# Seven-product feed-forward tiles: each product tied behind the one before it on the tensor engine

## The chip, the core and the metric

The kernel runs on one core of a Trainium2 chip. The metric is the device time of one execution in microseconds (us), as the median of three runs. The engines have short names in the profile: PE is the tensor engine (matrix products, called "products" here; PEld is its weight load), DVE the vector engine, ACT the scalar engine, POOL and SP the two engines that issue the transfers. Each engine works through a queue of its own in order and waits where an operand isn't ready.

## What is computed

One decoder layer on 512 tokens of width 1024, in float32: a SwiGLU feed-forward, a mixer (dilated attention beside a gated recurrence), and a second SwiGLU feed-forward, each between RMS norms. Only the feed-forwards matter here. The hidden width D_FF is 2816.

```python
def swiglu(x, w_gate, w_up, w_down):
    return (jax.nn.silu(x @ w_gate) * (x @ w_up)) @ w_down

f = swiglu(rms_norm(h, ffn1_norm_pre[l]), ffn1_w_gate[l], ffn1_w_up[l], ffn1_w_down[l])
h = h + 0.5 * rms_norm(f, ffn1_norm_post[l])
...
f = swiglu(rms_norm(h, ffn2_norm_pre[l]), ffn2_w_gate[l], ffn2_w_up[l], ffn2_w_down[l])
h = h + 0.5 * rms_norm(f, ffn2_norm_post[l])
```

## The kernel before

**Precision.** A float32 operand is split into a high and a low part (`split`, L269 on ACT for the high part, L270 on DVE for the low part), and a product of two operands is three matmuls: high by high, high by low, low by high. In a gate/up product these are L1008, L1009 and L1010, in a down step L922, L923 and L924. L923 is the first that needs the low part of the down weights, L1010 the first that needs the low part of the gate/up weights.

**Gate/up tiles.** The hidden width is cut into 22 tiles of 128 columns, numbered f = 0 to 21. In the first feed-forward tiles 0 to 5, in the second 0 to 3, are made by plain products. For each of the others, `prod` makes gate and up together by a scheme of seven half-size products instead of eight (a Strassen-like form): p1, p5, p6, p2, p7, p3, p4 in the order of the code, each 4 blocks of 128 by 3 matmuls, 12 matmuls of 256 columns. They accumulate in three banks of PSUM. Bank `b` (bank_73 or bank_74, by turns) takes p1, p6, p7 and p4; bank `y` (bank_75) a copy of `b` after p1 and then p2; bank `z` (bank_78) p5 and then p3. Between them ACT copies a bank out (`copy`, L1016, and L1029 for `b` to `y`) and DVE adds (`sum_of`, L1021): p6 and p7 may start only when the earlier content of `b` is copied, p3 only when p5's content of `z` is copied out, and p4 only when DVE has added p7's content of `b`.

**Down windows.** The down product is taken by seven products too, over groups of four tiles, called window groups a = 0 to 3. Its seven steps (`step`, L922 to L924, each 2 halves j = 0, 1 of 6 matmuls of 512 columns) run between the gate/up tiles in windows of one, two or three steps, listed in WINDOWS and LEAD. p1, p6, p7, p4 accumulate in bank_76 and bank_77, p2, p5, p3 in bank_79 and bank_80; after a step DVE adds a bank into the accumulator `facc` (L941, L939) or ACT copies it (L934). Three windows of the first feed-forward matter below: group 0's (p1, p2, p5) after tile 7, group 1's (p1, p2, p5) after tile 10 and group 1's (p6, p7) after tile 11. The down weights of the first two steps of a window are made (`down_form`: L269 on ACT, L270 on DVE) in the tile before it, behind that tile's last copy, by the edge `behind("copy")`; the third step's weights are made in the window.

**What sets the order.** A list scheduler places each engine's instructions by priority and by its own estimate of when operands are ready. The code can hold it with edges: `behind("PE")` makes what is traced in it come after the PE instruction noted last, in the order of the PE's queue. An edge on one engine's own queue costs no semaphore. Before, the first product of a tile (p1) and each down step had such an edge, and p5, p6, p2, p7, p3, p4 had none.

```python
            with behind("PE"):
                product("p1", b, True)
            ...
            product("p5", z, True)
            c5 = copy(z)
```

Of the kernel before, what the change touches and what calls it, by code (L numbers as in the profile page):

```python
# [154 lines left out]
def hybrid_layer(ctx: ExitStack, tc: tile.TileContext, xT: bass.AP, xN: bass.AP, wst: bass.AP,  # L155
                 first: bass.AP, rows: bass.AP, wdn: bass.AP, wbig: bass.AP, consts: bass.AP, bias: bass.AP, out: bass.AP):
    nc = tc.nc
    DVE, ACT, PE = nc.vector, nc.scalar, nc.tensor
# [121 lines left out]
    def tmp(name):  # L280
        return tpool.tile([P, T], F32, name=name, tag="t")
# [534 lines left out]
    def ffn(n, x, r, forms_x, home, pss):  # L816
# [80 lines left out]
        def down_form(a, p):  # L897
            w = wdt[home.n % 2]
            home.n += 1
            split(w[:, 0, :], w[:, 1, :], at[p])  # L900
            ready[p] = w
            q = NEXT[p]
            a += p in ("p7", "p3", "p4")
            if a < SEVEN:
                supply(a, q)
# [80 lines left out]
        @contextmanager  # L986
        def behind(*engines):
            with ExitStack() as es:
                for e in engines:
                    if e in last:  # L990
                        es.enter_context(tc.issue_after(last[e]))
                yield

        def prod(f, w, due):

            g = tmp("g")
            b, y, z = b_of[f % 2][:, :HB], y_[:, :HB], z_[:, :HB]
            u = ub[:, f % 4, :] if 4 < f < LAST[0] else tmp("u")
            if n == 1 and f in (6, 8):
                u = tmp("u")  # L1000

            def product(p, ps, start):
                if len(t[p][0].shape) == 4:
                    ps = ps.rearrange("q (b t) -> q b t", b=2)
                for k in range(4):
                    ks = slice(k * P, (k + 1) * P)
                    wh, wl, xh, xl = w[p][:, 0, ks], w[p][:, 1, ks], t[p][0][:, k], t[p][1][:, k]
                    PE.matmul(ps, wh, xh, start=start and k == 0, stop=False, skip_group_check=True)  # L1008
                    PE.matmul(ps, wh, xl, start=False, stop=False, skip_group_check=True)  # L1009
                    i = PE.matmul(ps, wl, xh, start=False, stop=k == 3, skip_group_check=True)  # L1010
                last["PE"] = i.ins

            def copy(ps):
                c = tpool.tile([P, HB], F32, name="c", tag="c", bufs=CB)
                with tc.high_priority(offset=EVAC):
                    last["copy"] = ACT.activation(c, ps, AF.Copy).ins  # L1016
                return c

            def sum_of(dst, ps, c):
                with tc.high_priority(offset=EVAC):  # L1020
                    DVE.tensor_add(dst, ps, c)  # L1021

            lead = f == n0
            with behind("PE"):
                product("p1", b, True)
            c1 = copy(b) if lead else None
            if not lead:
                with tc.high_priority(offset=EVAC):
                    ACT.activation(y, b, AF.Copy)  # L1029
            product("p5", z, True)  # L1030
            c5 = copy(z)
            product("p6", b, False)
            c6 = copy(b)
            product("p2", y, lead)
            if lead:
                sum_of(g[:, lo_], y, c1)
            with behind("copy"):
                for a, p in due:
                    down_form(a, p)
            product("p7", b, False)  # L1040
            sum_of(u[:, hi_], b, c5)
            with tc.high_priority(offset=EVAC):
                ACT.activation(g[:, lo_], g[:, lo_] if lead else y, AF.Silu)
            product("p3", z, False)
            sum_of(g[:, hi_], z, c6)
            product("p4", b, False)
            last["ACT"] = ACT.activation(g[:, hi_], g[:, hi_], AF.Silu).ins
            with tc.high_priority(offset=EVAC):
                DVE.scalar_tensor_tensor(u[:, lo_], g[:, lo_], -1.0, b, op0=ALU.mult, op1=ALU.mult)
            last["DVE"] = DVE.scalar_tensor_tensor(u[:, hi_], g[:, hi_], -1.0, u[:, hi_], op0=ALU.mult,  # L1050
                                                   op1=ALU.mult).ins
            return u
# [41 lines left out]
        for at_, ev in enumerate(order):  # L1094
# [16 lines left out]
            elif ev[0] == "prep":  # L1111
                with behind("DVE", "ACT"):
                    forms[ev[1]] = w_forms_in_place(("gu", n, ev[1]))
            elif ev[0] == "prod":
                due = order[at_ + 1]
                u = prod(ev[1], forms.pop(ev[1]), [(due[1], p) for p in due[2][:2]] if due[0] == "window" else [])
                if ev[1] == 4:
                    part0(u)
            elif ev[0] == "finish":
                finish(ev[1], u)  # L1120
            else:
                for i, p in enumerate(ev[2]):
                    with behind("PE"):
                        step(ev[1], p)
                    if len(ev[2]) > 2 and i == 0:
                        down_form(ev[1], ev[2][2])
# [612 lines left out]
```

## Time and profile before

| | before |
|---|---|
| median of three runs (lowest, highest) | 1225.02 us (1224.43 to 1225.36) |
| the profiled execution itself | 1224.49 us |
| span of the trace in it | 1222.7 us |
| PE busy | 1211.8 us, 99%, 7682 matmuls |
| DVE busy | 972.4 us, 80% |
| ACT busy | 736.5 us, 60% |
| granted clock of the tensor engine | 0.999 |
| the chain that ended last | PE 94%, DVE 4%, issue 1%, ACT 1% |

Matmuls are pipelined, so a matmul's row shows a longer time than it takes of the engine: rows of 0.28 us (256 columns) start 0.12 us after one another, rows of 0.39 us (512 columns) 0.23 us after one another. What the engine lost in a wait is therefore read from the starts.

### The profile page before, as it was taken

Reading aid. Unit: us, or ns where it says so; the run is one execution under the profiler, and the core shown is the slowest. Engines: PE = TensorE matmul, PEld = TensorE weight load, DVE = VectorE, ACT = ScalarE, POOL = GpSimd, SP = SyncE. Lnnn points to the kernel's source line nnn. Section 1 sums busy time; section 2 is a strip of 40 time slices with the busy share of each in tenths; the row PEclk is TensorE's granted clock in tenths of the full one; section 3 lists DMA queues with packets and bytes.
Section 4 is the critical chain, followed back from the end, with each engine's and each line's share of the span. In section 5 each row is a group of like instructions: output and inputs, shape, how many; then the busy total and the mean of one; then the engine's idle time right before and its main releaser. Section 6 shows DMA issues by size and latency. Waiting matters only on the chain.

```text
span 1222.7 us, 19286 instructions
## 1 busy us (share of the span) xinstructions
PE 1211.8 (99%) x7682; PEld 1099.0 (90%) x7682; DVE 972.4 (80%) x1513; ACT 736.5 (60%) x1221; POOL 82.1 (7%) x135
## 2 busy tenths in 40 slices
PE   9999999999999999999999999999999999999998
PEld 8888989999878899999998888888899999999996
DVE  7998778988579887888766798755788887979864
ACT  6566665665656564656665787724556665656552
POOL 0001101010102000000000000000110010101000
PEclk9999999999999999999999999999999999999999
DMA  6336546464735322222244234324463655555441
GB/s 247 138 104 172 162 115 166 136 166 127 253 122 175 107 81 102 78 79 104 70 140 151 88 121 155 129 99 164 143 190 108 162 154 147 156 139 160 117 155 69
DMA packets 37130, 166.57 MB, mean 136 GB/s; under 512 B 4144, under 2 KB 7600, under 8 KB 25008
## 3 DMA queue, kind: packets, MB, share of 16 engines
q1 hardware_dynamic: 18432, 107.13, 25.0%
q0 software_dynamic: 18608, 58.20, 18.0%
q8 instruction: 60, 0.98, 0.3%
q14 instruction: 30, 0.25, 0.1%
HBM read 153.26 MB, written 7.86 MB: 132 GB/s over the span
## 4 chain that ended last, share of the span: by engine, by line
PE 94%; DVE 4%; issue 1%; ACT 1%; DMA 0%; DVEq 0%; ACTq 0%
PE bank L1008 9%; PE bank L1009 9%; PE bank L1010 9%; PE bank L285 8%; PE bank L284 8%; PE bank L286 8%; PE bank L675 5%; PE bank L676 5%; PE bank L677 5%; PE bank L923 4%; PE bank L922 4%; PE bank L924 4%; PE bank L405 3%; PE bank L406 3%; PE bank L404 3%; DVE w L270 1%
## 5 line engine op out<-in xcount | busy, mean ns | idle before, releaser
L270 DVE TENSOR_TENSOR w<-raw,w 128x1024 fp32r<-128x1024 f32 (+1 forms) x272 | 297.0, 1102 | 69.1 <-ACT w L269 63.3
L269 ACT ACTIVATE w<-raw 128x1024 fp32r<-128x1024 f32 (+1 forms) x272 | 255.6, 959 | 97.0 <-PE bank L286 38.2
L1008 PE MATMUL bank<-big,w 128*128 128x256 f32 x816 | 233.9, 287 | 3.1 <-DVE u L1021 1.3
L1009 PE MATMUL bank<-big,w 128*128 128x256 f32 x816 | 230.7, 283 | 0.0
L1010 PE MATMUL bank<-big,w 128*128 128x256 f32 x816 | 229.4, 283 | 0.0
L1008 PEld LDWEIGHTS bank<-big,w 128*128 128x128 f32 x816 | 156.2, 191 | 8.3 <-DVE u L1021 2.0
L1009 PEld LDWEIGHTS bank<-big,w 128*128 128x128 f32 x816 | 156.3, 192 | 1.5
L1010 PEld LDWEIGHTS bank<-big,w 128*128 128x128 f32 x816 | 155.7, 192 | 0.0
L922 PE MATMUL bank<-wd,act 128*128 128x512 f32 x224 | 87.8, 392 | 0.0
L923 PE MATMUL bank<-wd,act 128*128 128x512 f32 x224 | 87.7, 392 | 0.0
L924 PE MATMUL bank<-wd,act 128*128 128x512 f32 x224 | 87.3, 390 | 0.0
L284 PE MATMUL bank<-big,w 128*128 128x512 f32 x176 | 68.5, 389 | 0.0
L285 PE MATMUL bank<-big,w 128*128 128x512 f32 x176 | 68.5, 389 | 0.0
L286 PE MATMUL bank<-big,w 128*128 128x512 f32 x176 | 68.5, 389 | 0.0
L675 PE MATMUL bank<-big,w 128*128 128x256 f32 x228 | 66.1, 290 | 0.0
L677 PE MATMUL bank<-big,w 128*128 128x256 f32 x228 | 64.7, 284 | 0.0
L286 PE MATMUL bank<-act,w 128*128 128x512 f32 (+1 forms) x184 | 64.7, 352 | 0.0
L285 PE MATMUL bank<-act,w 128*128 128x512 f32 (+1 forms) x184 | 64.7, 352 | 0.0
L284 PE MATMUL bank<-act,w 128*128 128x512 f32 (+1 forms) x184 | 64.6, 355 | 0.0
L676 PE MATMUL bank<-big,w 128*128 128x256 f32 x228 | 64.5, 283 | 0.0
L1016 ACT ACTIVATE c<-bank 128x256 f32<-128x256 f32 x70 | 26.6, 382 | 61.4 <-PE bank L1010 61.0
L270 DVE TENSOR_TENSOR wd<-npair,wd 128x1024 fp32r<-128x1024 f32 x24 | 29.3, 1223 | 39.2 <-ACT wd L269 39.2
(400 smaller groups left out, 3149.2 us busy)
## 6 DMA issues: line engine op xcount, KB each, us to landing
raw<-in_w SPq DMA_DIRECT2D x90, 1024.0 KB, 4.9
dr<-in_wdn POOLq DMA_DIRECT2D x40, 512.0 KB, 5.5
npair<-in_wdn POOLq DMA_DIRECT2D x32, 512.0 KB, 5.4
big<-act POOLq DMA_DIRECT2D x6, 512.0 KB, 3.7
h<-in_x SPq DMA_DIRECT2D x8, 256.0 KB, 4.9
h<-in_xn POOLq DMA_DIRECT2D x4, 512.0 KB, 5.2
raw<-in_wbig SPq DMA_DIRECT2D x2, 1024.0 KB, 4.8
kept_m<-h POOLq DMA_DIRECT2D x4, 512.0 KB, 2.9
```

Source lines behind the costliest of these rows:

```text
L269: ACT.activation(dh, src, AF.Copy)
L270: DVE.tensor_sub(dl, src, dh.bitcast(F32))
L284: PE.matmul(ps, wh, xh, start=first, stop=False)
L285: PE.matmul(ps, wh, xl, start=False, stop=False)
L286: PE.matmul(ps, wl, xh, start=False, stop=last)
L675: PE.matmul(ps, wh, xh, start=start and k == 0, stop=False, skip_group_check=True)
L922: PE.matmul(ps, xh, wh, start=start and k == 0, stop=False, skip_group_check=True)
L923: PE.matmul(ps, xh, wl, start=False, stop=False, skip_group_check=True)
L924: i = PE.matmul(ps, xl, wh, start=False, stop=k == 1, skip_group_check=True)
L1008: PE.matmul(ps, wh, xh, start=start and k == 0, stop=False, skip_group_check=True)
L1009: PE.matmul(ps, wh, xl, start=False, stop=False, skip_group_check=True)
L1010: i = PE.matmul(ps, wl, xh, start=False, stop=k == 3, skip_group_check=True)
```

## The change

The six products of a gate/up tile that had no edge get one: p5, p6, p2, p7, p3 and p4 are each put behind the last matmul of the product or step traced before. The block that makes the down weights stays where it was, between p2 and p7, behind the tile's last copy. Nothing is computed differently; no instruction is added or taken away.

```diff
-            product("p5", z, True)
+            with behind("PE"):
+                product("p5", z, True)
             c5 = copy(z)
-            product("p6", b, False)
+            with behind("PE"):
+                product("p6", b, False)
             c6 = copy(b)
-            product("p2", y, lead)
+            with behind("PE"):
+                product("p2", y, lead)
             if lead:
                 sum_of(g[:, lo_], y, c1)
             with behind("copy"):
                 for a, p in due:
                     down_form(a, p)
-            product("p7", b, False)
+            with behind("PE"):
+                product("p7", b, False)
             sum_of(u[:, hi_], b, c5)
...
-            product("p3", z, False)
+            with behind("PE"):
+                product("p3", z, False)
             sum_of(g[:, hi_], z, c6)
-            product("p4", b, False)
+            with behind("PE"):
+                product("p4", b, False)
```

On the tensor engine this moves instructions in three places of the first feed-forward, and two matmuls in each of five further windows. The first place is the window (p1, p2, p5) of group 0, between tiles 7 and 8. Here is the PE's order before, from the last matmul of step p2; bank_78 is `z`, w_756 holds tile 8's p5 weights and w_755 its p3 weights, wd_98 the weights of down step p5, bank_79 and bank_80 its two halves:

```order
L924 MATMUL bank_80<-wd_99,act 128x512
L922 MATMUL bank_79<-wd_98,act 128x512
L1008 MATMUL bank_78<-big,w_756 128x256
...
L922 MATMUL bank_80<-wd_98,act 128x512
L1010 MATMUL bank_78<-big,w_756 128x256
...
L1008 MATMUL bank_78<-big,w_755 128x256
...
L923 MATMUL bank_79<-wd_98,act 128x512
```

And now:

```order
L924 MATMUL bank_80<-wd_99,act 128x512
L922 MATMUL bank_79<-wd_98,act 128x512
L922 MATMUL bank_80<-wd_98,act 128x512
L923 MATMUL bank_79<-wd_98,act 128x512
L924 MATMUL bank_79<-wd_98,act 128x512
```

The scheduler had put 17 matmuls of tile 8 (all 12 of p5 and 5 of p3) between the first matmuls of down step p5; now these stand in tile 8, p5 behind p1 and p3 between p7 and p4. The second place, the window (p1, p2, p5) of group 1 between tiles 10 and 11, is alike: 20 matmuls of tile 11 (6, 6 and 8) move out of it. The third is tile 11 and the window (p6, p7) behind it, where 11 matmuls of tile 12's p5 stood ahead of tile 11's p4, and one of p5 and one of p3 between steps p6 and p7.

On the vector engine the rows of tile 11 and of the window behind it come in another order. Before (bank_74 is tile 11's `b`, wd_98 and wd_99 are the weights of steps p6 and p7, w_1415 and w_1414 tile 12's weights, w_1572 tile 13's):

```order
L1021 TENSOR_TENSOR g<-bank_78,c 128x256
L270 TENSOR_TENSOR w_1415<-raw,w_1415 128x1024
L270 TENSOR_TENSOR wd_98<-npair,wd_98 128x1024
L1021 TENSOR_TENSOR ub<-bank_74,c 128x256
L270 TENSOR_TENSOR w_1414<-raw,w_1414 128x1024
L270 TENSOR_TENSOR wd_99<-dr_100,wd_99 128x1024
...
L270 TENSOR_TENSOR w_1572<-raw,w_1572 128x1024
L941 TENSOR_TENSOR facc<-bank_76,facc 128x512
L941 TENSOR_TENSOR facc<-bank_77,facc 128x512
```

And now:

```order
L270 TENSOR_TENSOR wd_98<-npair,wd_98 128x1024
L270 TENSOR_TENSOR wd_99<-dr_100,wd_99 128x1024
L1021 TENSOR_TENSOR ub<-bank_74,c 128x256
L270 TENSOR_TENSOR w_1415<-raw,w_1415 128x1024
L1021 TENSOR_TENSOR g<-bank_78,c 128x256
L270 TENSOR_TENSOR w_1414<-raw,w_1414 128x1024
...
L941 TENSOR_TENSOR facc<-bank_76,facc 128x512
L270 TENSOR_TENSOR w_1572<-raw,w_1572 128x1024
L941 TENSOR_TENSOR facc<-bank_77,facc 128x512
```

Both splits of the down weights now stand ahead of the add that p4 waits for, and one weight split stands between the two adds of step p6. In the first two places the vector engine's order up to the split of the window's third step is unchanged; the queues that issue transfers are unchanged throughout.

## The prediction

> **What bounds the kernel now.** I read the page first: the busy times and the chain that ended last.
>
> ```profile
> PE 1211.8 (99%) x7682; PEld 1099.0 (90%) x7682; DVE 972.4 (80%) x1513; ACT 736.5 (60%) x1221; POOL 82.1 (7%) x135
> PE 94%; DVE 4%; issue 1%; ACT 1%; DMA 0%; DVEq 0%; ACTq 0%
> ```
>
> The tensor engine bounds the kernel nearly everywhere. The change neither adds nor removes a product, so it can only change how long PE waits. Next I asked the waits of the weight loads (PEld, the first of a product to stop) for 99 to 187 us, where the three changed places lie; columns: who waited for whom, us in total, times, the longest.
>
> ```profile
> PEld bank L1008 <- ACT c L1016: 1.9, 3, 0.8
> PEld bank L1008 <- DVE u L1021: 1.1, 1, 1.1
> PEld bank L1008 <- ACT bank L1029: 0.6, 3, 0.2
> PEld bank L923 <- DVE wd L270: 0.3, 1, 0.3
> PEld bank L1008 <- DVE ub L1021: 0.2, 1, 0.2
> ```
>
> That is 4.1 us, all there is to win. Each of the three waits for `c` is a product p3 that was pulled into a down window and stopped there for the copy of p5 out of bank `z`. Last, the timelines of the three engines (start, us, engine, instruction, and in brackets the idle time with its releaser). First place, PE:
>
> ```profile
> 99.13 0.39 PE L922 MATMUL bank<-wd,act 128*128 128x512 f32 x1
> 99.36 0.28 PE L1008 MATMUL bank<-big,w 128*128 128x256 f32 x1
> ...
> 100.31 0.40 PE L922 MATMUL bank<-wd,act 128*128 128x512 f32 x1
> ...
> 101.66 0.38 PE L1008 MATMUL bank<-big,w 128*128 128x256 f32 x1 [0.47 <-ACT c L1016]
> 101.88 0.28 PE L1009 MATMUL bank<-big,w 128*128 128x256 f32 x1
> 102.00 0.28 PE L1010 MATMUL bank<-big,w 128*128 128x256 f32 x1
> ...
> 102.35 0.40 PE L923 MATMUL bank<-wd,act 128*128 128x512 f32 x1
> ...
> 108.25 0.28 PE L1008 MATMUL bank<-big,w 128*128 128x256 f32 x1
> ...
> 111.38 0.28 PE L1010 MATMUL bank<-big,w 128*128 128x256 f32 x1
> 112.57 0.38 PE L1008 MATMUL bank<-big,w 128*128 128x256 f32 x1 [0.91 <-DVE u L1021]
> ```
>
> The starts give the rates: a 512-column product takes 0.23 us (99.13 to 99.36), a 256-column one 0.12 (101.88 to 102.00), and the first after a wait 0.10 more (101.66 to 101.88). From 99.36 to 102.35 PE ran the 17 pulled-up products of tile 8 (2.04 us) and one of the step (0.23); the rest of the 2.99 us, 0.7, is the wait for `c`. At the end of tile 8 p4 waited 112.57 − 111.38 − 0.12 = 1.07 us for the vector engine's add. The same place on DVE, and the copy on ACT:
>
> ```profile
> 99.40 0.69 DVE L941 TENSOR_TENSOR facc<-bank,facc 128x512 f32<-128x512 f32 x1
> ...
> 100.61 1.22 DVE L270 TENSOR_TENSOR wd<-npair,wd 128x1024 fp32r<-128x1024 f32 x1
> ...
> 112.09 0.42 DVE L1021 TENSOR_TENSOR u<-bank,c 128x256 f32<-128x256 f32 x1
> ```
>
> ```profile
> 101.22 0.38 ACT L1016 ACTIVATE c<-bank 128x256 f32<-128x256 f32 x1 [1.44 <-PE bank L1010]
> ```
>
> The copy ended at 101.60 and PE started at 101.66: an operand is seen 0.06 us after it is made.
>
> **The change part by part.** *What goes.* Of the 4.1 us the change removes every cause but the last row: p3 is no longer in a window, so its copy is long done (1.9); p5 stands between p1 and p6 in full, 12 × 0.12 = 1.44 us of cover for the copy of `b` (0.6 goes); PE comes to the down step behind tile 12 some 0.5 us later, with no more work ahead of its split, so it finds its weights made (0.3 goes). The 1.1 at tile 8's p4 is the open one. p4 needs the chain copy, two down splits, add, which runs from the end of p6. Before, the start of p2 (108.25) to p4 (112.57) was 4.32 us, and 27 products (12 of p2, 12 of p7, 3 of p3) filled 3.24 of it. Now all 12 of p3 stand there: 36 × 0.12 = 4.32, exactly the chain. Tile 9 already has that order:
>
> ```profile
> 123.92 0.28 PE L1008 MATMUL bank<-big,w 128*128 128x256 f32 x1
> ...
> 128.12 0.28 PE L1010 MATMUL bank<-big,w 128*128 128x256 f32 x1
> 128.23 0.38 PE L1008 MATMUL bank<-big,w 128*128 128x256 f32 x1
> 128.45 0.28 PE L1009 MATMUL bank<-big,w 128*128 128x256 f32 x1
> ```
>
> From its p2 (123.92) to its p4 (128.23) it is 4.31 us, no wait but the 0.10 of a restart. So I take 1.07 as gone at tile 8, with a restart left there, and of the last row's 0.2, tile 11's p4, one half. What goes: 1.9 + 0.6 + 0.3 + 1.07 + 0.1 = 4.0 us.
>
> *What comes, first place.* With the 17 products away, PE comes to the second half's L922 at 99.36. It needs that half's add into `facc`, done at 99.40 + 0.69 = 100.09: PE starts at 100.15, a wait of 0.79. Then L923 at 100.38 needs the low part of the weights: DVE ends it at 100.61 + 1.22 = 101.83, PE starts at 101.89, a wait of 1.51 and a restart of 0.10. DVE's queue up to there is unchanged and full of weight sums and adds, so nothing brings the split forward. Queued behind these products are the rest of the step and all of tile 8; the step's copies and DVE's next adds wait for them, none of which was late. Sum 2.4 us, against 0.7 before.
>
> *Second place*, the end of step p2 and step p5 of group 1, on PE, on ACT (the copies that give the two banks their content back) and on DVE:
>
> ```profile
> 150.67 0.39 PE L924 MATMUL bank<-wd,act 128*128 128x512 f32 x1
> ...
> 152.57 0.50 PE L922 MATMUL bank<-wd,act 128*128 128x512 f32 x1
> ...
> 154.25 0.40 PE L923 MATMUL bank<-wd,act 128*128 128x512 f32 x1
> ```
>
> ```profile
> 150.72 0.60 ACT L934 ACTIVATE bank<-s 128x512 f32<-128x512 f32 x1 [0.50 <-DVE facc L941]
> 151.92 0.60 ACT L934 ACTIVATE bank<-s 128x512 f32<-128x512 f32 x1 [0.60 <-DVE facc L941]
> ```
>
> ```profile
> 152.40 1.22 DVE L270 TENSOR_TENSOR wd<-npair,wd 128x1024 fp32r<-128x1024 f32 x1
> ```
>
> PE is free at 150.90. The first half's L922 can start at 151.32 + 0.06 = 151.38 (wait 0.48), the second half's at 152.58 (0.97 after the first one's 0.23), L923 at 153.62 + 0.06 = 153.68 (0.87, and 0.10). Sum 2.4 us. The chain behind the times is DVE's own work since tile 10's p6, so it moves along with PE.
>
> *Third place.* Steps p6 and p7 follow each other: p7's halves need DVE's two adds L941 of p6, with a weight split now between them. Before:
>
> ```profile
> 168.39 1.28 DVE L941 TENSOR_TENSOR facc<-bank,facc 128x512 f32<-128x512 f32 x2
> ```
>
> Counted from tile 11's p2: the add for p4 ends at 4.32 − 0.06 = 4.26 us, and then come three splits of 1.22, three small operations of at most 0.42 and the two adds, 1.28: 10.5 us in all. Rows overlap, the pair by 0.1 (1.28, where twice the single 0.69 is 1.38); 7 such overlaps make it 9.8. PE comes to p7's second half after 48 products of 0.12 and 18 of 0.23, 9.9 us. I take 0, with the 0.6 of rows that don't overlap as the upper bound.
>
> *Five small places.* In five (p6, p7) windows two products (0.24 us) leave the gap between p7's halves. The first of them, DVE then PE:
>
> ```profile
> 229.22 0.69 DVE L941 TENSOR_TENSOR facc<-bank,facc 128x512 f32<-128x512 f32 x1
> ```
>
> ```profile
> 230.00 0.28 PE L1008 MATMUL bank<-big,w 128*128 128x256 f32 x1
> ```
>
> The add ends at 229.91, seen at 229.97; PE will come at 230.00. So 0 each; the bounds are 0 and 0.24, five times 1.2 in all.
>
> *Sum.* What comes is 2.4 + 2.4 = 4.8 us, what goes 4.0. Net +0.8 us: the pulled-up products were paid for by almost as much waiting as they covered. On the profiled execution's own 1224.49 us that is 1225.3; on the median, 0.53 above it, 1225.8. About 0.2% (2.45 us) is what a measurement of this kernel can tell from no change.
>
> *Bounds.* Upper: the five places 1.2, the third place 0.6, tiles 8 and 11 0.1 each more: 1227.8. Lower: the nearest row for a wait of L923 on its split is 0.3 us, in the list above; if the two new ones were of that size, 1.8 us would not come: 1224.0. I take the DVE rows, which belong to these very splits.
>
> **The rivals.** *The vector engine falls behind (slower).* The cover of p4 has no slack: 4.32 us against 4.32. If the chain from p6 to the add is longer than 36 products at tiles 8, 11 and 12, p4 waits at each. For it: the 1.07 at tile 8 before, and DVE's rows at tile 11, now both splits ahead of the add. If all three wait as tile 8 did, 3 × 1.07 come on top: 1229.0. It decides the sign once the three lose 1.7 us together, 0.6 each. Against it: tile 9 has this order and waits for nothing.
>
> *No wait opens (faster).* If the down weights came in time at both places, the 4.0 would go and nothing come, 1221.0. Against it stand the two L270 rows, ending 2.2 and 2.3 us after PE would come to L923, in a queue that the change leaves alone there.
>
> *The clock.* The waits now lie together: 2.3 us of waiting in 2.5 us at the first place, 2.3 in 2.8 at the second. If the tensor engine's clock were halved after them until the end of p1, 10 products of 0.23 and 12 of 0.12, 3.7 us, would take 3.7 us more at each: 1233.2. By windows (us, busy times, PEclk, DMA share, GB/s) the clock didn't answer the waits that there are:
>
> ```profile
> 93.00:105.00 12.00, 11.53 (x63) 9.84 (x63) 11.82 (x18) 6.89 (x12) 2.30 (x3) 1.00 0.86 227
> 105.00:115.00 10.00, 9.09 (x70) 8.56 (x69) 7.61 (x10) 7.54 (x12) 1.41 (x2) 1.00 0.43 71
> ```
>
> The granted clock is 1.00 across the wait of 1.07 us. [...]
>
> *The edges do nothing.* If p5 and p3 had stayed where they were, it would be 1225.0; the order on PE shows that they move, so it has no share.
>
> **How the numbers follow.** The forecast has a chance of 0.80: the waits are read from rows of the same queues, and its bounds lie within 0.2% of 1225.0 but for the last 0.3 at the top, which needs every upper bound at once. The vector engine behind has 0.12, the clock 0.03, no wait 0.05. So faster 0.05, same 0.80, slower 0.15. The forecast's bounds, 1224.0 to 1227.8, hold 8 in 10 alone and are the range.
>
> **What would show it.** In the changed profile: the wait list of 99 to 187 us without `c` and nearly without L1029, with L923 on `wd` and L922 on `facc` and `bank` instead, 4 to 5 us in all; L923 of the first place at 101.9, p4 of tile 8 at 112.9 with no wait of over 0.2; p4 of tile 12 some 0.5 us later than before; and from 200 us on every row later by the same 0.8. A wait of p4 of over 0.6 at tiles 8, 11 and 12 makes the first rival right; L923 at the two places with no wait, the second; PEclk below 1.00, the third.

## The result and the profile after

The changed kernel took 1226.27 us (median of 22 executions, 1224.86 to 1230.13) against 1224.91 us of the kernel before (22 executions, 1223.85 to 1226.93): a ratio of 1.0013, 95% interval 1.0007 to 1.0019. That is 1.4 us slower, within the 0.2% that the prediction called "same", and 0.5 us above the predicted 1225.8. The profiled execution of the changed kernel took 1227.67 us, with a span of 1225.9 us, 3.2 us more than the span of before. It had a mean granted clock of 0.998, where the profile of before had 0.999.

The page of the changed kernel, its busy times and its chain that ended last:

```profile
PE 1213.1 (99%) x7682; PEld 1099.0 (90%) x7682; DVE 971.6 (79%) x1513; ACT 736.9 (60%) x1221; POOL 82.1 (7%) x135
PE 88%; DVE 7%; DMA 2%; issue 2%; ACT 1%; SPq 0%; DVEq 0%; ACTq 0%
```

PE does the same 7682 matmuls, and is busy 1.3 us longer with them. In the chain that ended last, DVE has 7% in place of 4% and the transfers (DMA) 2% in place of none. The waits of PE's weight loads in the same stretch, 99 to 188 us (who waited for whom, us in total, times, the longest), show where:

```profile
PEld bank L923 <- DVE wd L270: 2.5, 2, 1.5
PEld bank L922 <- ACT bank L934: 1.8, 2, 1.0
PEld bank L922 <- DVE facc L941: 1.3, 2, 1.0
```

All the waits of before are gone, those for `c`, `u`, `ub` and the copy of `b`. In their place stand the three that the prediction named. They add up to 5.6 us where it expected 4 to 5: the list counts from where a weight load stops, and that is ahead of the product's turn. By the starts of the products, below, the same waits are 4.6 us. PE's timeline at the first place, with the end of tile 8:

```profile
99.25 0.39 PE L922 MATMUL bank<-wd,act 128*128 128x512 f32 x1
100.26 0.49 PE L922 MATMUL bank<-wd,act 128*128 128x512 f32 x1 [0.63 <-DVE facc L941]
102.00 0.50 PE L923 MATMUL bank<-wd,act 128*128 128x512 f32 x1 [1.24 <-DVE wd L270]
102.33 0.40 PE L924 MATMUL bank<-wd,act 128*128 128x512 f32 x1
...
112.91 0.28 PE L1010 MATMUL bank<-big,w 128*128 128x256 f32 x1
113.03 0.38 PE L1008 MATMUL bank<-big,w 128*128 128x256 f32 x1
113.24 0.28 PE L1009 MATMUL bank<-big,w 128*128 128x256 f32 x1
```

The second half's L922 starts 1.01 us after the first half's, a wait of 0.78; L923 starts 1.74 us after that, a wait of 1.51, with a restart of 0.10. At tile 8, p4 (113.03) follows the last of p3 in its turn and pays only the restart.

The second place of the same execution:

```profile
151.08 0.39 PE L924 MATMUL bank<-wd,act 128*128 128x512 f32 x1
151.80 0.51 PE L922 MATMUL bank<-wd,act 128*128 128x512 f32 x1 [0.33 <-ACT bank L934]
153.00 0.50 PE L922 MATMUL bank<-wd,act 128*128 128x512 f32 x1 [0.69 <-ACT bank L934]
154.10 0.50 PE L923 MATMUL bank<-wd,act 128*128 128x512 f32 x1 [0.60 <-DVE wd L270]
...
155.37 0.63 PE L924 MATMUL bank<-wd,act 128*128 128x512 f32 x1
155.79 0.63 PE L923 MATMUL bank<-wd,act 128*128 128x512 f32 x1
...
157.93 0.41 PE L1008 MATMUL bank<-big,w 128*128 128x256 f32 x1
```

The waits are 0.49, 0.97 and 0.87 us. But then the products start 0.42 to 0.43 us after one another (155.37, 155.79), where the rate is 0.23, and their rows read 0.63 us instead of 0.39. No operand was waited for. The windows (us, busy times, PEclk, DMA share, GB/s) say what it is:

```profile
93.00:105.00 12.00, 10.13 (x50) 8.07 (x50) 11.82 (x19) 6.67 (x11) 2.30 (x3) 1.00 0.84 229
105.00:115.00 10.00, 10.00 (x83) 9.90 (x82) 7.36 (x10) 6.44 (x12) 1.41 (x2) 1.00 0.37 59
...
154.00:156.00 2.00, 1.90 (x6) 1.53 (x7) 1.25 (x3) 0.00 (x0) 0.86 (x1) 0.71 0.19 37
156.00:158.00 2.00, 2.00 (x6) 1.52 (x6) 0.00 (x0) 0.86 (x2) 0.00 (x0) 0.50 0.95 119
158.00:161.00 3.00, 3.00 (x26) 3.00 (x25) 0.69 (x1) 1.23 (x3) 0.00 (x0) 0.96 0.50 98
```

The granted clock fell to one half behind the second place. The clock lost is 2 × 0.29 + 2 × 0.50 + 3 × 0.04 = 1.7 us, which is 3.4 us at half speed. Behind the first place, with as much waiting, it stayed at 1.00.

What stands later, before and after, at the first matmul of the down window near 197 us:

```profile
197.03 0.40 PE L922 MATMUL bank<-wd,act 128*128 128x512 f32 x1
```

```profile
199.48 0.40 PE L922 MATMUL bank<-wd,act 128*128 128x512 f32 x1
```

The changed kernel is 2.45 us behind. 0.12 of it was there ahead of the first wait (99.25 against 99.13), some 1.6 is the half clock (8 starts from 154.67 to 157.93 in 3.26 us where 1.82 were due, and 0.15 in the two products behind), and 0.7 is left for the waits. The rest of the 3.2 us of span lies farther on. Each of the five small places costs 0.06 to 0.07:

```profile
232.23 0.39 PE L924 MATMUL bank<-wd,act 128*128 128x512 f32 x1
232.46 0.46 PE L922 MATMUL bank<-wd,act 128*128 128x512 f32 x1
232.75 0.39 PE L923 MATMUL bank<-wd,act 128*128 128x512 f32 x1
```

Here L922 came just too early for its add and L923 follows after 0.29 instead of 0.23; five of these make 0.3. The other 0.4 us is probably not the change's: near 312 us PE waits for a copy L1029 that stands on ACT behind a split L269 that waited 1.1 us for its transfer, in the profile of before 0.4. An experiment without any of the edges (earlyonly, below) lost 0.5 there. But the profile of before is the only one of ten without a wait there, and it is a single execution.

### The profile page after: what moved, and what is told of

It reads as the page before. It is cut to its first block, busy times and chain, and to the rows that moved or that the text cites. A ratio compares the mean times of both kernels' runs of the same rounds, so it can differ in the third digit from the quotient of the medians.

```text
span 1225.9 us, 19283 instructions
## 1 busy us (share of the span) xinstructions
PE 1213.1 (99%) x7682; PEld 1099.0 (90%) x7682; DVE 971.6 (79%) x1513; ACT 736.9 (60%) x1221; POOL 82.1 (7%) x135
## 4 chain that ended last, share of the span: by engine, by line
PE 88%; DVE 7%; DMA 2%; issue 2%; ACT 1%; SPq 0%; DVEq 0%; ACTq 0%
PE bank L1008 9%; PE bank L1009 9%; PE bank L1010 9%; PE bank L285 7%; PE bank L284 7%; PE bank L286 7%; PE bank L675 5%; PE bank L676 5%; PE bank L677 5%; PE bank L923 4%; PE bank L924 4%; PE bank L922 4%; PE bank L404 3%; PE bank L406 3%; PE bank L405 3%; DVE w L270 2%
## 5 line engine op out<-in xcount | busy, mean ns | idle before, releaser
L270 DVE TENSOR_TENSOR w<-raw,w 128x1024 fp32r<-128x1024 f32 (+1 forms) x272 | 297.7, 1104 | 69.2 <-ACT w L269 63.4
L269 ACT ACTIVATE w<-raw 128x1024 fp32r<-128x1024 f32 (+1 forms) x272 | 255.2, 959 | 96.0 <-PE bank L286 36.8
L923 PE MATMUL bank<-wd,act 128*128 128x512 f32 x224 | 88.5, 395 | 1.8 <-DVE wd L270 1.8
L922 PE MATMUL bank<-wd,act 128*128 128x512 f32 x224 | 88.7, 396 | 1.6 <-ACT bank L934 1.0
L270 DVE TENSOR_TENSOR wd<-npair,wd 128x1024 fp32r<-128x1024 f32 x24 | 29.4, 1224 | 44.2 <-ACT wd L269 44.2
```

The costliest lines, as they stand in the source:

```text
L269: ACT.activation(dh, src, AF.Copy)
L270: DVE.tensor_sub(dl, src, dh.bitcast(F32))
L922: PE.matmul(ps, xh, wh, start=start and k == 0, stop=False, skip_group_check=True)
L923: PE.matmul(ps, xh, wl, start=False, stop=False, skip_group_check=True)
```

## Experiments

Two theories stand against each other. *Waits alone* (W in the expectations): the new waits, net +0.8 us and something for the small places, are the whole of it, and what lies above that is scatter. *Waits and clock* (C): in a share of the executions the bunched waits also bring a half clock for 3.4 us, worth 1.6 to 1.7 us each time. One thing can be read without a run: built with the edge on p5 alone, the kernel has the same orders on PE, DVE and ACT as with all six. Once p5 is tied, the other five edges add nothing.

**The change once more.** This run and three of those below (idle products in both places, the early split, p3 tied) ran on one chip, the other four on another, each time beside the kernel before:

> The changed kernel once more, beside the three that follow. Theory W (waits alone): the order costs +0.8 us in every execution, and the half-clock stretch in its first profile was chance. Theory C (clock): the two bunched waits let the granted clock fall to 0.5 for 3.4 us in some executions, 1.7 us each time. W expects times in one bunch about 0.8 us above before; C expects a lower bunch some 0.8 above before at a clock of 0.999 or more, and others 1.5 to 4 us above that at 0.998 or less.

1227.26 us (1224.60 to 1229.05, 11 executions) against 1224.89 of before (33); ratio 1.0013, interval 1.0004 to 1.0022 (the ratios here are those on record and differ a little from the ratio of two medians). The executions fall into two groups. Seven had a mean clock of 0.996 to 0.998 and took 1227.23 to 1229.05, 1227.70 on average; four had 0.999 and took 1224.60 to 1226.21, 1225.70 on average. The profiled one (1227.82) had the half clock at the first place and not at the second:

```profile
102.00:105.00 3.00, 2.95 (x8) 2.34 (x9) 3.00 (x6) 0.60 (x1) 0.87 (x1) 0.59 0.67 182
105.00:115.00 10.00, 10.00 (x79) 9.74 (x78) 5.78 (x9) 6.31 (x10) 1.19 (x2) 0.95 0.24 46
150.00:154.00 4.00, 3.59 (x15) 2.39 (x13) 4.00 (x8) 2.75 (x5) 0.00 (x0) 1.00 0.83 264
154.00:158.00 4.00, 2.80 (x11) 2.10 (x12) 2.85 (x4) 1.15 (x2) 0.86 (x1) 1.00 0.75 135
```

The lost clock is 3 × 0.41 + 10 × 0.05 = 1.7 us again. The waits are the same in both executions, so whether the clock falls behind a bunch of them isn't set by the waits alone.

**Idle products in the gaps.** Eight matmuls whose results are thrown away stand between steps p2 and p5 in both places, so that PE works where it waited. They bring none of the operands sooner.

```diff
+                if p == "p5" and j == 0 and n == 1 and a in (0, 1):
+                    for _ in range(8):
+                        PE.matmul(banks[2], v[:, 0, 0, :P], w[:, 0, :T], start=True, stop=True)
```

> The changed kernel with 8 idle-work products of 512 columns (1.8 us, into the free bank y, results thrown away) put between steps p2 and p5 in both windows, where PE waits 2.3 us anyway. They lengthen nothing that ends last: L923 still waits 0.3 to 0.5 us for its split at both places. C expects the clock at 0.999 or 1.0 in every execution, no times more than 1 us above the lowest bunch, median 0.6 to 0.9 us above before. W expects the same spread and median as the changed kernel.

1225.93 us (1225.35 to 1227.96, 11 executions), ratio 1.0008, interval 0.9999 to 1.0017. Its waits, and the windows of the two places (by the starts of the products, L923 waits 0.47 and 0.50 us, as expected):

```profile
PEld bank L923 <- DVE wd L270: 1.5, 2, 0.8
PEld bank L922 <- DVE facc L941: 0.2, 1, 0.2
```

```profile
102.00:105.00 3.00, 3.00 (x21) 2.72 (x20) 2.81 (x6) 1.72 (x3) 0.41 (x1) 1.00 0.77 132
...
154.00:158.00 4.00, 4.00 (x28) 3.68 (x28) 1.10 (x2) 2.08 (x4) 0.49 (x1) 1.00 0.68 113
```

Six of the eleven executions had a clock of 0.999 and five 0.998; these five took 1225.38 to 1226.61, and none was at 1227 or over with less than 0.999 (the one of 1227.96 had 0.999). So theory C was right that no slow execution at a low clock is left, but four executions lie more than 1 us above the lowest, and the median is 1.0 above before where it said 0.6 to 0.9. Work that makes nothing took 1.3 us off the median of the changed kernel beside it (0.3 off that of its first run), and 7 of 11 such executions became 0 of 11: *waits alone* has no place for that. The 1.0 us that stays above before agrees with the waits, 0.7 at the two places and 0.3 at the five small ones; the idle products cover them but don't shorten them.

**Each place alone.** The same edit with `a == 0`, and with `a == 1`: one place filled, one bare.

> The changed kernel with the 8 idle products (512 columns, result thrown away) between steps p2 and p5 in the first place alone; the second place keeps its bare waits. Waits alone: nothing but waiting sets the time, so 1225.7 in every run, as with both places filled (1225.9). Clock: the second place alone can still bring the half clock. In the run of the unedited change 7 of 11 executions had it (1227.2 and over, mean clock 0.998 or less); if the two places bring it independently and alike, one place alone brings it in 1 - sqrt(4/11) = 0.4 of them: 3 to 6 of 11 executions at 1227 or over with a mean clock of 0.998 or less, the rest near 1225.6, a median of 1225.7 to 1226.5, none at 1229.

1226.31 us (1225.42 to 1228.09) against 1225.02 of before (31), ratio 1.0009, interval 1.0000 to 1.0018. Four of 11 executions took 1227.23 to 1228.09 at a clock of 0.997 or 0.998; the other seven, 1225.42 to 1226.35, had 0.999.

> The same 8 idle products (result thrown away) in the second place alone; the first place keeps its bare waits of 0.8 and 1.5 us. Waits alone: 1225.7 in every run. Clock: again 3 to 6 of 11 executions at 1227 or over with a mean clock of 0.998 or less, a median of 1225.7 to 1226.5; the half clock, where a profile shows it, falls in the first place (102 to 106 us) and never in the second.

1226.90 us (1225.83 to 1228.24) against the same 1225.02, ratio 1.0012, interval 1.0003 to 1.0020. Three of 11 took 1227.86 to 1228.24 at 0.998. The count hit and the median missed, by 0.4 us. Its profiled execution took 1227.98 at 0.999, with no half clock inside, at the bare place neither, but with one wait near 73 us, in another part of the kernel; the list gives it 1.8 us and puts it down to "issue", and by the starts it is 1.55. So the half clock is not the only thing that sets an execution back by 2 us, and a single time tells nothing; the clock beside it does.

Taken together: with both places bare, 14 of 33 executions were at 1227 or over with a clock of 0.998 or less (7 of the first 22, 7 of 11); with one place bare, 7 of 22; with none, 0 of 11. Of the 86 executions of the kernel before, 3 were. These counts are rough. The profiles of before and of the first run of the change also end at half clock, for the last 2.0 and 2.7 us of the span, which alone takes 0.0008 and 0.0011 off the mean; the fall inside, 3.41 us, takes 0.0014 off it. The kernel before has 0.998 at ordinary times too (1224.92 and 1224.98 us), so 0.998 by itself shows nothing. Three more of the first 22 had 0.997 or 0.998 at 1226.30 to 1226.98. Counted by 0.997 or less alone, it is 10 of 33 with both places bare, 3 of 22 with one (all three with the second place bare), 0 of 11 with none, and 1 of the 64 executions of the kernel before whose clock is on record. That filling both places takes the falls away is shown; what each place brings by itself is not.

**Where the clock fell.** This was read afterwards, and no run was made to test it. In the first profile of the change the granted clock went from 1.00 to 0.50 at 154.84 us and back at 158.25, 3.41 us later; in the second it fell at 102.51 and was back near 106. Stretches of 3.41 or 3.42 us at the two places, in the first profile and then in the second:

```profile
100.22:103.63 3.41, 2.13 (x8) 1.56 (x9) 3.41 (x5) 0.17 (x1) 0.87 (x1) 1.00 0.91 258
151.42:154.84 3.42, 1.79 (x6) 1.03 (x6) 3.42 (x6) 0.93 (x2) 0.37 (x1) 1.00 0.87 180
```

```profile
99.10:102.51 3.41, 1.55 (x6) 0.76 (x5) 3.34 (x5) 0.63 (x1) 0.07 (x1) 1.00 0.93 219
153.71:157.12 3.41, 2.12 (x8) 1.39 (x8) 3.14 (x5) 0.60 (x1) 0.86 (x1) 1.00 0.71 149
```

In the stretch that ends at the fall, PE's rows (their ends are modelled) leave 3.42 − 1.79 = 1.63 us idle in the first profile and 3.41 − 1.55 = 1.86 in the second. At the place where the clock stayed at 1.00, the stretches shown leave 1.28 and 1.29 us. But that depends on where a stretch is laid: at the first place of the first profile, 99.00 to 102.41 us leaves 3.41 − 1.54 = 1.87 idle, and the clock stayed at 1.00 there and behind it. What decides between executions with the same waits was not shown. In the profile of the kernel before, the clock is 1.00 up to 1216 us, and the longest wait there is the 1.07 us of `u`.

**The split made early.** If the waits are what DVE's queue makes them, the cure is on DVE: the split of the window's third step stood behind weight sums that nobody was waiting for. It gets a higher priority.

```diff
-                        down_form(ev[1], ev[2][2])
+                        with tc.high_priority(offset=EVAC):
+                            down_form(ev[1], ev[2][2])
```

> The changed kernel with the split of a window's third down weights put ahead of the gate/up weight sums on the vector engine (high priority for that one call). If the waits at L923 and L922 are DVE's queue, as the prediction said, they fall from 2.4 us to about 0.7 at the first place and to about 0.9 at the second: both theories expect 3.0 to 3.3 us less than the changed kernel's lower bunch, about 1222.4. C expects also no run at a clock under 0.999, since no wait is left of over 0.6 us; W makes no difference there.

1222.81 us (1222.01 to 1224.51, 11 executions), ratio 0.9983, interval 0.9974 to 0.9992. Its waits in the same stretch:

```profile
PEld bank L923 <- DVE wd L270: 1.1, 2, 0.8
PEld bank L922 <- ACT bank L934: 1.0, 2, 0.7
PEld bank L922 <- DVE facc L941: 0.2, 1, 0.2
```

2.3 us of waits by the list instead of 5.6 (by the starts 0.7 us at the first place and 0.9 at the second, as expected), and no execution more than 1.7 us above the median. Against the lower group of the changed kernel (1225.70) it is 2.9 us less, where 3.0 to 3.3 were expected; three executions had a clock of 0.998, none of them slow. The forecast of the wait terms from rows L270 holds: with the rows moved, the waits go.

**p3 tied, p5 left free.** The edge on p3 alone: p5's products still cover the two gaps, and p3 no longer stands in a window waiting for its copy.

```diff
             product("p5", z, True)
...
+            with behind("PE"):
+                product("p3", z, False)
```

> The edge on p3 alone: p5 stays in the windows as cover (12 products, 1.44 us), p3 goes back between p7 and p4, so that nothing in the window waits for the copy of bank z. New: p6 follows p1 directly at tiles 8 and 11 and waits about 0.7 us for the copy of bank b. Waits of 0.9 + 0.1 + 0.7 at each place, 3.4 us against 4.8 of the changed kernel and 4.0 that before had: 1224.2, some 0.6 us below before. C: no run under a clock of 0.999.

1224.16 us (1223.28 to 1226.67, 11 executions), ratio 0.9993, interval 0.9984 to 1.0002. The waits were 3.1 us in place of 4.1 of before:

```profile
PEld bank L923 <- DVE wd L270: 1.8, 2, 0.9
PEld bank L1008 <- ACT bank L1029: 1.3, 2, 0.7
```

The time agrees with what was expected, but the interval holds 1. Theory C expected no clock under 0.999; one execution had 0.998 and one 0.997 (1226.67). What slowed the last is open, as it was not profiled: the profile taken (1223.54) has a granted clock of 1.00 at both places (99 to 115 and 150 to 158 us), where its longest wait is 0.9 us.

**The early split without the edges**, on the kernel before:

> The kernel before, without the edges, with the third step's weights split early as in the run named early. If the early split and the edges need one another: PE's pulled-up products cover the split already, only the 0.3 us of L923 at the second place goes and the waits for c, u and the copy to y stay: 1224.5 to 1224.9, no change that can be measured. Rival, the early split is worth its 3 to 4 us with or without the edges: 1221.5. A third outcome, a new order of the tensor engine's queue because the scheduler sees the weights earlier: then fewer products are pulled up and it lies between.

1221.70 us (1220.21 to 1225.30, 10 executions) against 1225.02 of before (31), ratio 0.9971, interval 0.9961 to 0.9981. The expectation was wrong and its rival right as to the time; the way there is that of its third outcome, fewer products pulled up. All that is left of the waits of before:

```profile
PEld bank L1008 <- DVE ub L1021: 0.5, 1, 0.5
PEld bank L1008 <- ACT bank L1029: 0.3, 1, 0.3
```

4.1 us of waits became 0.8, and the time fell by 3.3. The reason is on PE (first place), with the split on DVE behind it:

```profile
99.71 0.28 PE L1008 MATMUL bank<-big,w 128*128 128x256 f32 x1
99.83 0.40 PE L923 MATMUL bank<-wd,act 128*128 128x512 f32 x1
```

```profile
98.29 1.22 DVE L270 TENSOR_TENSOR wd<-npair,wd 128x1024 fp32r<-128x1024 f32 x1
```

The split ends at 99.51, 2.3 us sooner than in the kernel before (2.0 beside PE, which is 0.36 us earlier in this execution). The scheduler now pulls up 7 products of tile 8 where it had pulled 17, all of them p5, so none has to wait for a copy. At the second place it pulls 9 instead of 20. This is the fastest version of the study: faster than the kernel before by 0.29%, than the changed kernel by more.

**The early split with p3 tied:**

> The edge on p3 alone (p5 still pulled up into the two windows) and the early split. With p3 tied the two L923 waits were 0.9 us each and two restarts of 0.1; the early split ends 1.2 us sooner at the first place and 2 us sooner at the second, so both go: 1224.2 - 2.0 = 1222.2, with p6's two waits of 0.6 us behind the copy to y left. If the scheduler, seeing the weights earlier, no longer pulls p5 into the windows, it becomes the early run again: 1222.8. Both waits are too short for the half clock: no execution at a mean clock under 0.998.

1221.80 us (1221.06 to 1225.22, 10 executions), ratio 0.9972, interval 0.9963 to 0.9981: the same as without the edge. At the two places no p3 product is pulled up any more, so there the edge holds nothing. The expected 1222.2 left waits of 0.6 us at p6; they were 0.3 and less. The profiled execution was the slowest (1225.22), and it shows a half clock from another cause, at tile 11:

```profile
160.91 0.28 PE L1010 MATMUL bank<-big,w 128*128 128x256 f32 x1
162.95 0.38 PE L1008 MATMUL bank<-big,w 128*128 128x256 f32 x1 [1.77 <-DVE ub L1021]
...
165.24 0.63 PE L923 MATMUL bank<-wd,act 128*128 128x512 f32 x1
165.67 0.63 PE L924 MATMUL bank<-wd,act 128*128 128x512 f32 x1
```

```profile
164.00:166.00 2.00, 2.00 (x9) 1.81 (x8) 2.00 (x5) 1.60 (x3) 0.00 (x0) 0.52 0.89 170
166.00:168.00 2.00, 2.00 (x7) 1.53 (x6) 0.55 (x2) 0.81 (x2) 0.00 (x0) 0.63 1.05 334
```

In this execution ACT's split of the down weights waited 1.8 us for its transfer, DVE's splits and add stood behind it, and p4 waited 1.9 us. Here the clock fell behind one wait of 1.9 us: the clock lost is 2 × 0.48 + 2 × 0.37 = 1.7 us. The expectation put no mean clock under 0.998, and none was, yet a half clock is there: the mean is too coarse a sign.

## Why the prediction was right, and where it was not

*Where PE waits, and how long: right at the two places.* Forecast for the first place 0.79, 1.51 and 0.10, measured 0.78, 1.51 and 0.10. For the second 0.48, 0.97, 0.87 and 0.10, measured 0.49, 0.97, 0.87 and 0.10. L923 of the first place was forecast at 101.9 and p4 of tile 8 at 112.9; less the 0.12 by which this execution ran late from the start, they came at 101.88 and 112.91. That the waits follow DVE's rows was then shown by moving one of them: 5.6 us of waits became 2.3, and the median fell by 4.5 us (1227.26 to 1222.81), 3.3 by the waits; the rest agrees with the half clock, of which its executions show no sign (no clock under 0.998).

*What goes: right.* p4 of tile 8 waits for nothing but its restart, so 36 products do cover its chain, and no wait for `c`, `u` or the copy is left in the stretch. The rival of the vector engine falling behind needed waits of over 0.6 us at tiles 8, 11 and 12; the list shows none. One sign was wrong in itself: the step behind tile 12 was to come 0.5 us later, where the prediction's own terms give 4.8 − 3.7 = 1.1. It came 0.9 later (183.85 against 181.28, less 0.12 and the 1.6 of the half clock).

*The net of 0.8 us: right at the row, a little low for the kernel.* At 199.48 us the waits had cost 0.7. The third place was put at 0 with a bound of 0.6, and the small places at 0 with a bound of 0.24 each; the third place cost a short restart (0.07, within the 0.7), the small ones 0.3 in all. That makes 1.0 us of waiting. What goes was priced by the list of weight-load waits and what comes by the starts; single terms differ (the 0.3 of L923 is a restart of 0.10 by the starts), and that they cancel is luck. The 16 executions at a clock of 0.999 or over, of both runs of the change, have a median of 1225.5, 0.6 above before; with the gaps filled it was 1.0 above. The forecast of 0.8 lies between.

*The clock: the step that failed is the weight of this rival, and its price.* The rival had 0.03, on the argument that the clock stayed at 1.00 across a wait of 1.07 us. That row is no evidence for bunches of 2.3 us; no wait in the profile of before is longer. By time and clock it happened in about 14 of 33 executions, and two profiles show it. Its price, every product to the end of p1 at half rate, 3.7 us at each place and 1233.2 in all, was the author's estimate, and no run shows it. Measured, the half clock lasted 3.4 us and cost 1.6 to 1.7 us; at one place in each of the two profiled executions, at both in neither (the slowest, 1230.13 and 1229.05 at 0.996, may have had both; they were not profiled). So the half clock that the rival supposed was there, and its 1233.2 was not. On a median it counts by its share: with 7 of 22 executions hit the median was 1226.27, with 7 of 11 it was 1227.26, both in the range, and the prediction's 1225.8 is near what the executions gave that were not hit (1225.5). That the first median came within 0.5 us of it is in part luck, since it hangs on how many executions are hit.

*That the edges do what they say:* with p5 tied alone the order is the same, so the change is that one edge. (The edge on p3 alone does move p3, as the run with p3 tied shows.)

## What to carry to other kernels

Pulled-up work in a gap is a sign that an operand comes late. Look for what makes the operand late before you forbid the pulling: here one split moved ahead of work that nobody waited for gained 3.3 us, while tying the products gave back the waits that they had covered. Price a wait by the engine's own rows, and look at its neighbours in time and at the granted clock behind them: waits that were forecast to 0.01 us, 2.3 us of them within 2.5 to 2.8 us, cost 1.6 to 1.7 us more in the executions where the clock fell to one half for 3.4 us.

## What the runs showed of the hardware

In the first profile of the change the granted clock of the tensor engine fell to 0.50 for 3.41 us (154.84 to 158.25) behind 2.3 us of waiting within 2.8 us, 0.74 us after PE was at work again (154.10), and stayed at 1.00 behind 2.3 us of waiting within 2.5 us at the first place. In the second profile, with the same waits, it fell at the first place (mean clock 0.59 from 102 to 105 us) and stayed at 1.00 at the second. In the run of the early split with p3 tied it fell behind a single wait of 1.9 us (mean clock 0.52 from 164 to 166 us, 0.63 from 166 to 168), about 1.1 us after PE was at work again (162.95). Each fall lost 1.7 us of clock. Single waits of 1.07 us (the kernel before, 1.00 from 105 to 115 us) and 1.55 us (the second place filled, mean clock 0.999) went by without a fall inside, and so did the gaps that idle products filled down to 0.5 us (1.00 from 102 to 105 and from 154 to 158 us).
